# A fifth split place in the attention overlays, small sum jobs in the merge gates, and stored block sums, in a Strassen-Winograd decoder layer

## Chip, core and metric

The kernel runs on one core of one Trainium2 chip. The metric is the device time of one execution in microseconds. The engines are named as in the profile: PE (TensorE's matmuls), PEld (its weight loads), DVE (VectorE), ACT (ScalarE), POOL (GpSimd) and SP (SyncE, whose queue issues nearly all DMAs).

## What is computed

One decoder layer on 2048 tokens with 1024 features, in float32, batch and depth 1:

```python
mod = silu(c) @ w_ada + b_ada;  shift, scale, gate = split(mod, 3)
u = x * (1 + scale) + shift
q, k, v, a_gate, p_in, p_gate, m_a, m_p = split(u @ w_in)
a = (sliding_window_sink_attention(q, k, v, sinks, rel_bias) * silu(a_gate)) @ w_attn_proj
p = ((group_linear(multiscale_causal_pool(p_in), w_pool_mix) * pool_scale) * silu(p_gate)) @ w_pool_proj
y = ((sigmoid(m_a) * a + sigmoid(m_p) * p) @ w_out) * (1 + gate)
x = layer_norm(alpha * x + y, ln_gain, ln_bias)
```

There are 16 query heads of 64 and 2 key-value heads, a window of 128 tokens, and causal pools over 2, 4, 8 and 16 tokens.

## The kernel before

**Quads.** Every large matrix product is cut into quads: 256 output features by 1024 tokens (one chunk, `s` = 0 or 1), summed over 1024 input features. A quad is one step of the Strassen-Winograd scheme: seven block products instead of eight, named B11, T1, T2, B21, T3, B22, T4 after the set of the second operand that they read. A set is four tiles of 128 x 512, each split into a high and a low part that TensorE takes at full speed; a product is 4 x 3 matmuls of 512 columns (high by high, high by low, low by high, `mm3`, line 142), so 12 PE instructions. `sets` holds all seven sets of one operand in SBUF; when an operand is done, `turn_sets` (line 540) loads the next one's from DRAM and splits it, one set after another.

**Weights of a quad.** `Quad.load_w` (line 262) loads four blocks of 128 x 512 into a tile W and a fifth into A22. `sum1` (274), `mid` (277) and `late` (282) form sums and differences in W on POOL. Before its products a quad's blocks pass through four splits, stages F (products B11, T1), S (T2, B21), Th (T3, B22) and L (T4): ACT casts the high part (`split_part` part 0), DVE, or POOL for Th of unpaired quads, subtracts it for the low part (part 1). The parts stand in tiles `w_set`.

**The order of the work** is a table made by `plan` (line 352): 518 products in a row, and for each product which splits, loads and sums are issued ahead of it. F, S and Th need two places for `w_set` tiles, L one. A ring of four places serves all stages; a phase whose pools have `wx` places of its own uses those as well, and its splits may stand three products ahead instead of two (line 405). A part whose place is freed only by the product just ahead is put right at its own product (lines 418 and 419). Each engine executes its instructions in this program order. Small work is hung between products by `at`, `steps` and `defer` (lines 327 to 342), in ticks of one product.

**Phases.** For each chunk: the chunk start (`g0`, `g1`: keys and values, the first quads of q and gates, in pairs; products 0 to 27 and 175 to 202), the overlay (`o0`, `o1`: 13 unpaired quads, 91 products, 28 to 118 and 203 to 293, between whose matmuls `overlay` (746) sets the attention steps) and the merge gates (`e0`, `e1`: 8 paired quads, 56 products, 119 to 174 and 294 to 349, with the pooling by `pool_job`, 980). Then come the projections for chunk 0 and 1 (112 products) and the output product (56). `c` (line 203) hands out tiles for results from a ring of four, with `more` places where the phase has them.

**The attention step** (845) is 12 PE instructions: four scores (`lg`), four transposes (`pt`), four value products (`pv`); with a minimum, a scaling, a low part and two sums on DVE, two exponentials, a scaling, a cast and a copy on ACT.

**Small jobs.** `fold_parts` (1050) multiplies W_in's pool columns with the pool mix in chunk 0's start: 16 pieces of 12 matmuls, written to `wmix_d` through tiles of `c`. `sums_job` (945) forms the seven sets of u for chunk 1 in eight jobs (u_B, u_T in the profile) during chunk 0's overlay; `second_start` (1360) forms those of w_out times the gate in chunk 1's start with tiles `spare` of 128 x 1024 (`sums_to`, 224).

## Time and profile before

| | us |
|---|---|
| Median of 3 runs (lowest to highest) | 1837.79 (1834.65 to 1840.94) |
| The profiled execution's own time | 1841.62 |
| Its span, first to last instruction | 1839.8 |
| PE / DVE / ACT / POOL busy in it | 1705.4 / 1302.6 / 940.8 / 683.6 |
| Mean granted clock of PE | 0.972 |

Times in the profile are microseconds unless marked ns. A row of the timeline is start, duration, engine, operation with output<-inputs and shapes, and in brackets the engine's idle time before it with what ended that. In a group row the two numbers behind the bar are total busy time and mean ns of one, then the idle time before them. A row of the windows view is a stretch, its length, the busy time of each engine with the number of instructions, the granted clock, the DMA engines' mean busy share and GB/s. All helpers are called through one line, so every row says L56 and is told apart by its tiles.

### The profile page before, as it was taken

To read this page: it belongs to the slowest core of one execution; us is meant where nothing else is said; L and a number is where in the kernel's file an instruction comes from. 1 tells how busy PE (TensorE), PEld (TensorE's weight loads), DVE (VectorE), ACT (ScalarE), POOL (GpSimd) and SP (SyncE) were. 2 spreads that over 40 slices of the span, in tenths; PEclk is the share of its full clock that TensorE was granted. 3 is DMA by queue.
4 is the path that set the end of the run, shared out by engine and by line. 5 is a ranking of instruction groups with operands and counts; after the bars stand their busy time and mean duration, and the time that the engine had idled before them with its cause. 6 is when DMAs were issued, how large, how long until landed. Compare 5 with 4: busy or idle time off the path is not lost.

```text
span 1839.8 us, 24893 instructions
## 1 busy us (share of the span) xinstructions
PE 1705.4 (93%) x8061; PEld 1407.7 (77%) x8061; DVE 1302.6 (71%) x2309; ACT 940.8 (51%) x1796; POOL 683.6 (37%) x618
## 2 busy tenths in 40 slices
PE   6897799898989999989998999899999999999996
PEld 5686678777877887867886878688878888888785
DVE  5854578677763877757786877557786876879778
ACT  3543577666662435526675767434363444434452
POOL 3021345353534232473342444433232333323452
PEclk9899899999999999999999999999999999999998
DMA  8486646555533779595354544257785684778342
GB/s 332 139 264 214 177 153 190 185 179 188 169 129 129 233 237 349 193 334 176 123 166 139 172 130 150 99 163 227 237 306 202 235 284 158 251 247 290 137 149 103
DMA packets 223267, 365.13 MB, mean 198 GB/s; under 512 B 21776, under 2 KB 78880, under 8 KB 223136
## 3 DMA queue, kind: packets, MB, share of 16 engines
q1 hardware_dynamic: 221056, 359.55, 59.1%
q10 hardware_dynamic: 2048, 3.96, 0.7%
q8 instruction: 64, 1.05, 0.2%
q14 instruction: 67, 0.55, 0.1%
q0 software_dynamic: 32, 0.02, 0.0%
HBM read 235.50 MB, written 131.10 MB: 199 GB/s over the span
## 4 chain that ended last, share of the span: by engine, by line
PE 48%; DVE 14%; ACT 10%; issue 8%; DMA 7%; POOL 4%; SPq 1%; POOLq 0%; DVEq 0%; ACTq 0%
PE mm L56 29%; PE lg L56 9%; PE c L56 7%; DVE w_set L56 5%; ACT L L56 3%; ACT w_set L56 2%; DVE wide L56 2%; PE pv L56 2%; PE pt L56 1%; POOL W L56 1%; DVE L L56 1%; POOL st L56 1%; DMA qs<-q_d 1%; DVE ptl L56 1%; SPq L56 1%
## 5 line engine op out<-in xcount | busy, mean ns | idle before, releaser
L56 PE MATMUL mm<-set_B,w_set 128*128 128x512 f32 x2664 | 657.1, 393 | 4.8 <-DVE w_set L56 3.0
L56 PEld LDWEIGHTS mm<-set_B,w_set 128*128 128x128 f32 x2664 | 499.3, 190 | 110.8 <-DVE w_set L56 5.0
L56 PE MATMUL mm<-set_T,w_set 128*128 128x512 f32 x1824 | 480.0, 407 | 60.3 <-DVE w_set L56 38.5
L56 POOL TENSOR_TENSOR W<-W 128x512 f32<-128x512 f32 x216 | 315.6, 1476 | 464.8 <-DVE w_set L56 309.2
L56 PEld LDWEIGHTS mm<-set_T,w_set 128*128 128x128 f32 x1824 | 345.7, 195 | 155.1 <-DVE w_set L56 59.0
L56 DVE TENSOR_TENSOR w_set<-W,w_set 128x1024 fp32r<-128x1024 f32 x196 | 258.4, 1319 | 135.6 <-ACT w_set L56 110.1
L56 ACT CAST w_set<-W 128x1024 fp32r<-128x1024 f32 x222 | 232.2, 1047 | 196.5 <-POOL W L56 181.0
L56 POOL TENSOR_TENSOR W<-W,A 128x512 f32<-128x512 f32 x72 | 103.6, 1439 | 389.8 <-DMA A<-in_win_dram 187.6
L56 PE MATMUL c<-set_T,w_set 128*128 128x512 f32 x864 | 214.2, 397 | 8.4 <-DVE w_set L56 5.9
L56 PE MATMUL lg<-set_T,w_set 128*128 128x512 f32 x864 | 212.4, 394 | 4.8 <-ACT w_set L56 2.2
L56 PEld LDWEIGHTS c<-set_T,w_set 128*128 128x128 f32 x864 | 163.8, 191 | 46.2 <-DVE w_set L56 8.4
L56 PEld LDWEIGHTS lg<-set_T,w_set 128*128 128x128 f32 x864 | 163.0, 190 | 42.1 <-ACT w_set L56 3.1
L56 ACT ACTIVATE L<-L,nm 128x257 f32<-128x257 f32 (+1 forms) x256 | 126.8, 498 | 19.4 <-DVE nm L56 19.1
L56 DVE CUSTOM_DVE_ANT_0 L<-lg,bt,nsink 128x256 f32<-128x256 f32 (+1 forms) x256 | 111.0, 470 | 18.5 <-PE lg L56 16.9
L56 DVE TENSOR_SCALAR L<-L,sm 128x256 f32<-128x256 f32 (+1 forms) x128 | 114.3, 893 | 4.5
L56 ACT ACTIVATE L<-L,sm 128x256 f32<-128x256 f32 (+1 forms) x128 | 64.2, 502 | 101.6 <-DVE sm L56 101.6
L56 DVE TENSOR_TENSOR ptl<-pt,pth 128x512 fp32r<-128x512 f32 (+1 forms) x128 | 85.9, 671 | 34.5 <-ACT pth L56 33.7
L56 ACT CAST pth<-pt 128x512 fp32r<-128x512 f32 (+1 forms) x128 | 72.2, 564 | 56.2 <-PE pv L56 55.8
L56 PEld LDWEIGHTS lg<-kk,qs 128*128 128x128 f32 x512 | 79.2, 194 | 25.0 <-issue 10.4
L56 ACT ACTIVATE sig<-mm 128x512 f32<-128x512 f32 x76 | 45.4, 598 | 96.9 <-PE mm L56 86.0
L56 PE MATMUL lg<-kk,qs 128*128 128x256 f32 (+1 forms) x512 | 84.6, 289 | 9.7 <-DMA qs<-q_d 8.0
L56 DVE TENSOR_TENSOR w_set<-A,w_set 128x512 fp32r<-128x512 f32 x74 | 61.4, 830 | 34.1 <-ACT w_set L56 19.1
(205 smaller groups left out, 2026.0 us busy)
## 6 DMA issues: line engine op xcount, KB each, us to landing
W<-in_win_dram SPq DMA_DIRECT2D x40, 512.0 KB, 5.6
qs<-q_d SPq DMA_DIRECT2D x128, 128.0 KB, 4.0
W<-in_win_dram SPq DMA_DIRECT2D x46, 256.0 KB, 4.5
A<-in_win_dram SPq DMA_DIRECT2D x42, 256.0 KB, 5.5
ag_d<-sig SPq DMA_DIRECT2D x32, 256.0 KB, 3.9
q_d<-q_hi SPq DMA_DIRECT2D x32, 256.0 KB, 3.5
q_d<-q_lo SPq DMA_DIRECT2D x32, 256.0 KB, 3.6
pg_d<-sig SPq DMA_DIRECT2D x32, 256.0 KB, 3.9
```

What stands on the lines that cost most here:

```text
L56: return lambda *args, **kw: self.tc.keep_in_program_order(op(*args, **kw))
```

## The change

1. The overlays' pools get one `w_set` place of their own (`wx=1`), so `plan` uses five and issues splits up to three products ahead.
2. The eight jobs for u move from chunk 0's overlay to its merge gates, every 4.5 products; the sums of w_out become eight such jobs of half the width in chunk 1's merge gates, every 5.5 products, and leave chunk 1's start. `ux` gets two tiles.
3. For 31 of the quads chunk 0 stores the sum of `sum1` and the second difference of `mid` in `sums_d` (two stores of 256 KB each); chunk 1's quad of the same weights loads both in one DMA of 512 KB in place of one block and leaves the two POOL operations out.
4. The fold runs in 16 consecutive products, from the tenth on, and its result tiles come from ring `x`; the banks of the value transposes are swapped.
5. The results' ring has five tiles in chunk 0's merge gates and four in chunk 1's (six before), and six in chunk 1's start (four before), whose `spare` ring has five instead of seven.

What moves on DVE, in chunk 0's overlay at product T2 of the quad ag[6] (the row `mm<-mm,p` is the sum that follows T2; ISA is the minimum with its readout; `w_set<-W` is the low part of stage S). Before:

```order
L56 SCALAR_TENSOR_TENSOR q_lo<-mm,q_hi 128x512
L56 TENSOR_TENSOR w_set<-W,w_set 128x1024
L56 RECIPROCAL sm<-sm 128x2
L56 TENSOR_SCALAR L<-L,sm 128x256
L56 ISA L,nm<-lg,bt,nsink 128x256
L56 ISA nm 128x1
L56 ISA L,nm<-lg,bt,nsink 128x256
L56 ISA nm 128x1
L56 TENSOR_TENSOR ptl<-pt,pth 128x512
L56 TENSOR_TENSOR st<-pv,o_4159 64x128 x2
L56 TENSOR_TENSOR mm<-mm,p_4130 128x512
```

Now, two attention steps earlier, at the result of the quad before:

```order
L56 TENSOR_TENSOR st<-pv,o_3919 64x128 x2
L56 SCALAR_TENSOR_TENSOR q_lo<-mm,q_hi 128x512
L56 TENSOR_TENSOR w_set<-W,w_set 128x1024
L56 RECIPROCAL sm<-sm 128x2
L56 TENSOR_SCALAR L<-L,sm 128x128
```

The low part of S stood one attention step ahead of the sum behind T2, that is, at T2 itself; now two more steps lie between, and the place where it stood holds none.

What moves on SP, in chunk 0's merge gates behind the weights of the third group's first quads (`pg_d`, `mp_d` and `ma_d` hold gates, `vb` and `pin_` belong to the pooling, DMAHW and the engine names are the semaphores waited for). Before:

```order
L56 DMA A_5842<-in_win_dram 128x512 [waits DMAHW3_49]
L56 DMA pg_d<-sig 128x512 [waits DMAHW4_49,DVE_49]
L56 DMA vb<-px_d 128x528 [waits DMAHW5_49,DVE_49]
L56 DMA pg_d<-sig 128x512 [waits DMAHW6_49]
L56 DMA pin_T_109<-st 128x512 [waits DMAHW7_49,DVE_49]
L56 DMA pg<-pg_d 128x512 [waits DMAHW0_49]
```

Now:

```order
L56 DMA A_5767<-in_win_dram 128x512 [waits DMAHW5_49]
L56 DMA u_T_82<-ux 128x256 [waits DMAHW6_49,Pool_49]
L56 DMA u_T_86<-ux 128x256 [waits DMAHW7_49,Pool_49]
L56 DMA u_T_84<-ux 128x256 [waits DMAHW0_49,Pool_49]
L56 DMA u_B_80<-ux 128x256 [waits DMAHW1_49,Activation_49]
L56 DMA u_B_83<-ux 128x256 [waits DMAHW2_49,Activation_49]
L56 DMA u_B_85<-ux 128x256 [waits DMAHW3_49]
L56 DMA ux<-in_xt_dram 128x2x256 [waits DMAHW6_49,DMAHW7_49,DMAHW4_49,DMAHW0_49]
L56 DMA ux<-in_xt_dram 128x2x256 [waits DMAHW5_49]
L56 DMA pg_d<-sig 128x512 [waits DVE_49]
L56 DMA sums_d<-W 128x512 [waits Pool_49]
L56 DMA vb<-px_d 128x528 [waits DVE_49]
```

A job's six stores and two loads stand between the weights and the gates' stores, and the first load waits for the landing of the three u_T stores just ahead. Counted in the same order, from three rows ahead of the stage's first gate load (`pg<-pg_d`) to the first load of the next operand's sets, SP issues 178 DMAs with 41.0 MB in chunk 0's merge gates (96 with 26.8 MB before) and 164 with 39.3 MB in chunk 1's (96 with 26.9).

What moves on PE, at the end of chunk 0's start (`pv<-spare` and `pt<-spare` are folds). Before:

```order
L56 MATMUL lg<-set_T_560,w_set 128x512 x12
L56 MATMUL mm<-set_B_569,w_set 128x512 x12
L56 MATMUL pv<-spare,room_w 128x256 x12
L56 MATMUL c_970<-set_T_560,w_set 128x512 x12
L56 MATMUL pt<-spare,room_w 128x256 x12
L56 MATMUL mm<-set_B_569,w_set 128x512 x12
L56 MATMUL pv<-spare,room_w 128x256 x12
L56 MATMUL lg<-set_T_642,w_set 128x512 x12
L56 MATMUL pt<-spare,room_w 128x256 x12
L56 MATMUL c_970<-set_T_642,w_set 128x512 x12
```

Now:

```order
L56 MATMUL lg<-set_T_561,w_set 128x512 x12
L56 MATMUL pv<-spare,room_w 128x256 x12
L56 MATMUL mm<-set_B_570,w_set 128x512 x12
L56 MATMUL pt<-spare,room_w 128x256 x12
L56 MATMUL c_959<-set_T_561,w_set 128x512 x12
L56 MATMUL pv<-spare,room_w 128x256 x12
L56 MATMUL mm<-set_B_570,w_set 128x512 x12
L56 MATMUL pt<-spare,room_w 128x256 x12
L56 MATMUL lg<-set_T_635,w_set 128x512 x12
L56 MATMUL c_959<-set_T_635,w_set 128x512 x12
```

The gap after the third fold of four is gone and the last fold ends one product earlier.

The diff, without the removed `sums_to` and `second_start` and without repeated forms:

```diff
+    sums_d = dp.tile([36, P, 2, CH], F32, name="sums_d")
...
-        def __init__(self, srcs, consume):
-            self.srcs, self.consume = srcs, consume
+        def __init__(self, srcs, consume, sums=None, again=False):
+            self.srcs, self.consume, self.sums, self.again = srcs, consume, sums, again
...
-            q.dma_start(x[:, 2, :], self.srcs[1][:, 0:CH])
+            if self.again:
+                q.dma_start(x[:, 1:3, :], self.sums)
+            else:
+                q.dma_start(x[:, 2, :], self.srcs[1][:, 0:CH])
...
             e.tensor_tensor(x[:, 1, :], x[:, 1, :], x[:, 0, :], ALU.subtract)
-            e.tensor_tensor(x[:, 2, :], x[:, 0, :], x[:, 2, :], ALU.subtract)
+            if not self.again:
+                e.tensor_tensor(x[:, 2, :], x[:, 0, :], x[:, 2, :], ALU.subtract)
+
+        def keep_sum(self, n):
+            if self.sums is not None and not self.again:
+                sp.dma_start(self.sums[:, n, :], self.w[:, 1 + n, :])
...
             q.mid(pool)
+            defer(2, lambda q=q: q.keep_sum(1))
...
-                    z.sum1()
+                    if not z.again:
+                        z.sum1()
+                        defer(1, lambda z=z: z.keep_sum(0))
...
-            vtp = bank(("pt", "pv")[t]).rearrange("p (b a d) -> p b a d", b=NB, a=2)
+            vtp = bank(("pv", "pt")[t]).rearrange("p (b a d) -> p b a d", b=NB, a=2)
...
-        return Quad((win[TQ + m], win[TQ + m + 1]), consume)
+        return Quad((win[TQ + m], win[TQ + m + 1]), consume, sums_d[1 + m // 2], s == 1)
...
-    def sums_job(ph, i, c):
+    def sums_job(ph, store, i, c, load, scale):
...
-            u = job["u"] = ph.t.tile([P, 4, C2], F32, tag="ux", bufs=1, name="ux")
+            u = job["u"] = ph.t.tile([P, 4, C2], F32, tag="ux", bufs=2, name="ux")
...
+    def input_sums(ph, first):
...
+        for n in range(8):
+            steps(first, 1 + 4.5 * n, sums_job(ph, u1_d, n // 2, n % 2, load, scale))
+
+    def output_sums(ph, first):
...
+        def scale(u, k):
+            dve.tensor_tensor(u, u, row[0], ALU.mult)
+
+        for c in range(2):
+            at(first + 1 + 22 * c, lambda c=c: gate_cols(c))
+            for i in range(4):
+                steps(first, 1 + 5.5 * (4 * c + i), sums_job(ph, wo_d, i, c, load, scale))
...
-            st = ph.c("st").rearrange("p (m e d) -> p m e d", m=2, e=2)
+            st = ph.own("st").rearrange("p (m e d) -> p m e d", m=2, e=2)
...
-            first = base + 4 + 5 * g
+            first = base + 6 + 4 * g
...
-                    at(p - 2, lambda g=g: split_mix(g))
+                    at(p - 1, lambda g=g: split_mix(g))
...
-            if s == 0:
-                for n in range(8):
-                    steps(first, 1 + 11 * n, sums_job(ph, n // 2, n % 2))
...
+            (output_sums if s else input_sums)(ph, phase["first"])
...
-            phase(Pools("g1", spare=7, wx=2), start, second_start)
-        phase(Pools(f"o{s}", pv=2), alone, middle(s))
-        phase(Pools(f"e{s}", pg=2, st=8, more=2, wx=2), end, finish_chunk(s, ain_d[0] if s else u1_d))
+            phase(Pools("g1", spare=5, wx=4, more=2), start, second_start)
+        phase(Pools(f"o{s}", pv=2, wx=1), alone, middle(s))
+        phase(Pools(f"e{s}", pg=2, st=8, more=1 - s, wx=2), end, finish_chunk(s, ain_d[0] if s else u1_d))
```

`sums_job` keeps its ten steps over nine products: load at 0, scaling at 3 and 4, stores of B11, B21 and B22 at 5, differences on POOL at 5, 7 and 8, the other stores at 6 and 9.

72 lines of the change are left out of this document (21 added, 51 removed).

## The prediction

> **What bounds the kernel now.** I read the windows view first, cut at the program's stages: chunk start (first row), overlay of chunk 0, merge gates of chunk 0, then the same three of chunk 1.
>
> ```profile
> core 0: us, PE busy (x) PEld busy (x) DVE busy (x) ACT busy (x) POOL busy (x), PEclk, DMA share, GB/s
> 23.80:172.70 148.90, 126.00 (x619) 104.43 (x620) 90.67 (x150) 66.24 (x112) 17.48 (x11) 0.92 0.67 223
> 172.70:572.70 400.00, 360.18 (x1830) 297.98 (x1829) 268.98 (x676) 253.09 (x596) 179.63 (x194) 0.96 0.56 172
> 572.70:725.40 152.70, 152.50 (x673) 125.89 (x671) 112.64 (x140) 63.50 (x92) 44.36 (x39) 1.00 0.71 237
> 725.60:814.30 88.70, 81.10 (x346) 64.82 (x347) 61.70 (x57) 36.47 (x51) 52.90 (x32) 0.98 0.78 274
> 814.30:1203.40 389.10, 360.04 (x1862) 299.44 (x1861) 271.08 (x672) 246.04 (x579) 157.55 (x163) 0.97 0.47 150
> 1203.40:1356.00 152.60, 152.59 (x674) 126.00 (x672) 112.65 (x140) 63.49 (x92) 43.05 (x31) 1.00 0.74 238
> ```
>
> The merge gates are PE at its limit: 673 matmuls in 152.70 us, 0.227 us each and no idle. That is the price of one 512-column matmul, and 12 of them, one product, cost 2.72. An overlay has 91 products, 1092 matmuls, 247.8 us. Its other PE instructions (1830 - 1092 = 738 and 1862 - 1092 = 770) come in attention steps of 12. The timeline of PE gives a step as 434.68 - 433.30 = 1.38 us:
>
> ```profile
> 433.30 0.64 PE L56 MATMUL lg<-kk,qs 128*128 128x256 f32 x4
> 434.68 1.54 PE L56 MATMUL mm<-set_B,w_set 128*128 128x512 f32 x6
> ```
>
> So the overlays need 247.8 + 61.5 x 1.38 = 332.7 and 247.8 + 64.2 x 1.38 = 336.4 us, and take 67.3 and 52.7 more. The waits of PE in each (total, times, longest) name the cause, first three rows chunk 0, last two chunk 1:
>
> ```profile
> PE mm L56 <- DVE w_set L56: 20.7, 12, 2.6
> PE mm L56 <- ACT w_set L56: 8.2, 8, 2.1
> PE lg L56 <- DMA qs<-q_d: 6.9, 2, 6.7
> PE mm L56 <- DVE w_set L56: 17.9, 10, 2.8
> PE mm L56 <- ACT w_set L56: 6.2, 7, 2.1
> ```
>
> PE waits for the weights' high and low parts, about once per quad. The timelines of PE, DVE and POOL show one case, the T2 product of ag[6]:
>
> ```profile
> 420.90 3.37 PE L56 MATMUL mm<-set_T,w_set 128*128 128x512 f32 x14
> 426.81 0.50 PE L56 MATMUL mm<-set_T,w_set 128*128 128x512 f32 x1 [2.53 <-DVE w_set L56]
> 424.61 2.15 DVE L56 TENSOR_TENSOR w_set<-W,w_set 128x1024 fp32r<-128x1024 f32 x1
> 424.41 1.26 POOL L56 TENSOR_TENSOR st<-st 128x512 f32<-128x512 f32 x1
> ```
>
> DVE begins the low part at 424.61, after the product before (T1) has let go of its place, and PE resumes 0.05 us after it ends.
>
> **The fifth place.** The order shows that this low part now stands two attention steps earlier on DVE, so the 2.53 us go, as do the other waits for w_set. What is late next? Two quads of the windows view, one without and one with the wait:
>
> ```profile
> 262.80:290.90 28.10, 27.78 (x154) 23.38 (x153) 23.48 (x57) 20.48 (x52) 12.72 (x15) 1.00 0.56 164
> 411.95:444.95 33.00, 29.82 (x153) 24.89 (x153) 25.15 (x63) 21.44 (x54) 12.60 (x14) 0.95 0.60 202
> ```
>
> By the prices a quad needs 84 x 0.227 + 70/12 x 1.38 = 27.1 us. The first loses 1.0, the second 5.9, of which only 2.5 is the named idle: the clock fell to 0.95 and matmuls beside a gap stand alone. The Trainium skill, TensorE: Matmul & The Clock Gate, Part 1, lets the clock fall to half only after an idle window of about 3.4 us; by it waits of at most 2.8 us would cost no clock. The 0.95 beside a 2.53 us wait says otherwise, so I go by the whole excess; what the page's reading would give is a rival below.
>
> Not recoverable: the wait for qs, whose loads the change leaves where they stand:
>
> ```profile
> 200.40 1.19 PE L56 MATMUL lg<-kk,qs 128*128 128x256 f32 x4 [6.75 <-DMA qs<-q_d]
> ```
>
> The four scores behind it take 1.19 instead of the 0.64 at 433.30, so the clock was low too: I set 9 us in chunk 0, 2 in chunk 1. That leaves 58 and 51. After the change a quad still loses something, since DVE is busy 23.5 to 25.2 us of 27.1. From the rows: at least 1.0; if DVE can't be used over 23.48 / 28.10 = 84%, a quad with 25.15 takes 30.1, a loss of 3.0. I take 1.2, near the quad that ran, over 13 quads 15.6 per overlay: gains of 42 and 35, **77 us**. Ends: 109 with no loss, 55 with 2.1 (midway).
>
> **Chunk start, the fold.** Its products now follow one another without a gap and its result tiles leave the ring of four that q's and the gates' results use. PE around the last folds, and one wait of ACT among them:
>
> ```profile
> 148.33 0.50 PE L56 MATMUL pt<-spare,room_w 128*128 128x256 f32 x2 [1.39 <-ACT room_w L56]
> 160.05 0.63 ACT L56 ACTIVATE sig<-p 128x512 f32<-128x512 f32 x1 [5.12 <-DMA q_d<-q_hi]
> 161.21 2.93 PE L56 MATMUL pv<-spare,room_w 128*128 128x256 f32 x12 [7.93 <-ACT st L56]
> 168.37 1.70 PE L56 MATMUL pt<-spare,room_w 128*128 128x256 f32 x12 [1.24 <-ACT st L56]
> 169.91 2.91 PE L56 MATMUL c<-set_T,w_set 128*128 128x512 f32 x12
> ```
>
> From 148.33 to 169.91 (21.6 us) stand three folds and two products, which cost 3 x 1.54 (169.91 - 168.37) + 2 x 2.72 = 10.1 undisturbed. Some 11.5 are lost, 13 with the wait ahead, and ACT waited there for a store of a tile of that ring to land. I take **10**; ends 0 (the queue that delays the stores still waits for the gate sums) and 13.
>
> **Chunk 1's start.** The sums of w_out leave it. It needs 28 x 2.72 = 76.3 and takes 88.70. DVE's timeline, and PE's wait:
>
> ```profile
> 786.77 1.23 DVE L56 TENSOR_TENSOR spare<-spare,cb 128x1024 f32<-128x1024 f32 x1 [7.23 <-DMA spare<-in_wout_dram]
> 787.92 1.22 DVE L56 TENSOR_TENSOR w_set<-W,w_set 128x1024 fp32r<-128x1024 f32 x1
> PE c L56 <- DVE w_set L56: 3.8, 1, 3.8
> ```
>
> DVE stood for w_out's load with splits behind it. That goes: **6** of the 12 (the idle and a low clock after it); ends 3 and 9.
>
> **The merge gates take the small jobs.** Prices of what moves, and of what the stored sums spare:
>
> ```profile
> L56 POOL TENSOR_TENSOR ux<-ux 128x256 f32<-128x256 f32 x32 | 25.6, 811 | 3.0 <-ACT ux L56 2.9
> L56 ACT ACTIVATE ux<-ux,mod 128x512 f32<-128x512 f32 x16 | 12.8, 807 | 0.0
> L56 DVE TENSOR_TENSOR spare<-spare,cb 128x1024 f32<-128x1024 f32 x8 | 12.6, 1596 | 9.6 <-DMA spare<-in_wout_dram 9.6
> L56 DVE TENSOR_TENSOR w_set<-W,w_set 128x1024 fp32r<-128x1024 f32 x196 | 258.4, 1319 | 135.6 <-ACT w_set L56 110.1
> ```
>
> In chunk 0's gates POOL goes from 44 to 70 of 152.7 us and ACT from 64 to 76: covered. In chunk 1's, DVE goes from 112.7 to 125; and beside POOL a split took 2.15 instead of 1.32, so 32 small POOL operations can lengthen DVE's work by up to 32 x 0.83 = 27, to 152 of 152.6. The Trainium skill, SBUF — State Buffer, Who interferes with whom, calls this an exclusive port that a two-input DVE operation and GpSimd hold in turn; the 2.15 agrees.
>
> The DMAs are the nearer limit. Up to the first load of the next sets (46 products, 125 us) the order has 178 DMAs with 41.0 MB in chunk 0's gates where it had 96 with 26.8: 327 GB/s for 214. The densest stretch before, and an ordinary one:
>
> ```profile
> 680.00:698.00 18.00, 18.00 (x81) 14.92 (x80) 13.01 (x15) 8.70 (x13) 8.61 (x7) 1.00 0.73 248
> 716.00:734.00 18.00, 15.95 (x67) 11.94 (x65) 12.23 (x13) 8.40 (x12) 6.54 (x4) 1.00 1.05 401
> ```
>
> 401 GB/s is reached, with PE 2 us short. So 327 fits, with little spare, and the sets' turn follows at once. SP is also held: a job's load goes into a tile whose stores were issued just before, so SP stands for a landing, with weight loads queued behind it; those stand three products (8.2 us) ahead of their split, which is the cover. The results' ring shrinks from six tiles to five and four; a tile is stored two products after it is made and its landing takes 3.9 us:
>
> ```profile
> ag_d<-sig SPq DMA_DIRECT2D x32, 256.0 KB, 3.9
> ```
>
> That is 9.3 of the 10.9 us that four products give. And DVE, as at 786.77, can again stand for w_out, now with three products of cover instead of two. All of this is hidden on average and not in every burst: I take **+4** for each of the two stages with what follows it; ends 0 and +18.
>
> **Stored sums.** Chunk 1 saves two POOL operations in each of 31 quads; POOL is not what PE waits for, so 0. Chunk 0 stores 62 tiles of 256 KB, spread over its stages: 0, with a rival below. The swapped banks of the value transposes and the smaller rings of chunk 1's start change no count and no order that PE waits for: 0.
>
> **Sum.** The profiled execution took 1841.62 us (span 1839.8, 1.8 around it; 3.8 above the median of the runs shown, inside their scatter): 1841.6 - 77 - 10 - 6 + 8 = **1757**. Below 0.3%, 5.5 us, a change can't be told from none.
>
> **Rivals.**
> DVE takes PE's place in the overlays: 2.1 lost per quad, gain 55 instead of 77: **1779**. For it: 84% at the quickest quad. Against: that quad still kept up. 0.15.
> The merge gates starve: PE is short by 2 in 18 us, as at 716, over 2 x 153 us: 34 instead of 8: **1783**. 0.12. Both: **1805**, 0.04.
> Only the named idle returns (28.9 and 24.1, less the 31 kept): gain 22, **1812**. It is the clock page's reading as well; the quad at 411.95 speaks against it. 0.04.
> No loss per quad and no price in the gates: 1841.6 - 109 - 12 - 8 = **1713**. 0.04.
> The splits wait for their own inputs instead, so the place gives nothing: 1841.6 - 16 + 8 = **1834**. 0.03.
> Slower: in chunk 0 the difference that overwrites a stored sum must wait on POOL until the store has landed, with the second split's input behind it. If PE saw that landing in all 31 quads, 31 x 3.9 = 121: 1757 + 121 = **1878**. It decides from 85 / 31 = 2.7 us per quad. Against: two to three products lie between store and difference in the overlays, and the second split stands four products later in the paired stages. 0.03.
> The forecast keeps 0.55.
>
> **Numbers.** Range 1730 (1.0 lost per quad or less, no price in the gates) to 1793 (past the two single rivals). Faster by over 0.3%: 0.55 + 0.15 + 0.12 + 0.04 + 0.04 + 0.04 and a third of the 0.03 = 0.95; within 0.02; slower 0.03.
>
> **What would show it.** Right: overlays of about 358 and 354 us with under 5 us of PE waiting for w_set in each; the chunk start about 139; chunk 1's start about 83; the gates 153 to 160 with DMA near 0.95. DVE as the bound shows as PE waiting for nm, ptl or w_set with DVE over 84% busy there; starving gates as PE idle there behind DMAs of W or A; the slower case as POOL's W<-W waiting for sums_d. I am wrong if the overlays keep more than 370 us or the gates exceed 165.

## The result, and the profile after

The changed kernel takes 1810.52 us in the median of four runs (1806.00 to 1817.08), beside 1836.22 of the kernel before on the same chip: a ratio of 0.986, interval 0.9822 to 0.9898. It is faster, by some 26 us where 80 were forecast, and lies above the range (1730 to 1793). The profiled execution is the slowest of the four, 1817.08 us, its span 1815.3.

The windows view of the changed kernel, cut at the same products as before (to some 0.4 us): chunk 0's start, overlay and merge gates, then chunk 1's (columns as in the prediction's first rows). The last row is one quad of chunk 0's overlay, ag[6], which took 33.00 us before.

```profile
23.60:168.70 145.10, 129.10 (x618) 107.31 (x619) 90.28 (x152) 69.21 (x115) 16.54 (x12) 0.92 0.71 242
168.70:534.40 365.70, 346.89 (x1830) 293.32 (x1830) 262.69 (x675) 239.55 (x577) 160.81 (x162) 0.98 0.56 174
534.40:731.30 196.90, 166.86 (x674) 132.95 (x672) 111.43 (x140) 74.71 (x109) 70.47 (x69) 0.90 0.79 264
731.30:811.70 80.40, 78.33 (x345) 63.92 (x346) 46.97 (x50) 38.22 (x53) 19.27 (x13) 1.00 0.54 187
811.70:1169.40 357.70, 345.05 (x1862) 294.08 (x1861) 263.80 (x670) 243.62 (x578) 125.80 (x134) 1.00 0.52 168
1169.40:1332.00 162.60, 154.64 (x675) 125.55 (x673) 122.80 (x156) 63.67 (x93) 56.48 (x48) 0.99 0.90 304
395.30:423.80 28.50, 27.58 (x153) 23.57 (x152) 23.71 (x63) 20.74 (x52) 11.52 (x13) 1.00 0.64 215
```

Against the rows of before:

| stage | before | forecast | after | difference | forecast difference |
|---|---|---|---|---|---|
| chunk 0's start | 148.9 | 139 | 145.1 | -3.8 | -10 |
| chunk 0's overlay | 400.0 | 358 | 365.7 | -34.3 | -42 |
| chunk 0's merge gates | 152.7 | 157 | 196.9 | **+44.2** | +4 |
| chunk 1's start | 88.7 | 83 | 80.4 | -8.3 | -6 |
| chunk 1's overlay | 389.1 | 354 | 357.7 | -31.4 | -35 |
| chunk 1's merge gates | 152.6 | 157 | 162.6 | +10.0 | +4 |

The six differences sum to -23.6, and the span fell by 24.5. The overlays gave 65.7 of the 77 that were forecast. Two thirds of the miss (40 of 61 us) stand in chunk 0's merge gates, where PE hardly idled before (152.50 of 152.70 us busy). PE's waits there now (total, times, longest):

```profile
PE mm L56 <- ACT w_set L56: 27.9, 5, 11.0
PE mm L56 <- DVE w_set L56: 1.2, 3, 0.5
```

There are five waits for the high part of the weights, up to 11.0 us long, and a granted clock of 0.90 beside them. One of them is followed here from end to end, in the third group of pairs. First PE's timeline, the T3 products of the group before, at which the weights of the third group's two quads are due (in the order, their loads stand ahead of the first and the third of these rows), and the wait itself:

```profile
601.95 2.88 PE L56 MATMUL lg<-set_T,w_set 128*128 128x512 f32 x12
604.67 2.88 PE L56 MATMUL mm<-set_B,w_set 128*128 128x512 f32 x12
607.39 2.88 PE L56 MATMUL c<-set_T,w_set 128*128 128x512 f32 x12
...
640.26 5.89 PE L56 MATMUL mm<-set_B,w_set 128*128 128x512 f32 x12 [10.98 <-ACT w_set L56]
```

Then SP's issues:

```profile
610.74 1.08 SPq L56 DMA_DIRECT2D W<-in_win_dram  x2
611.86 0.62 SPq L56 DMA_DIRECT2D A<-in_win_dram  x1
...
613.80 1.87 SPq L56 DMA_DIRECT2D u_T<-ux  x3
621.09 1.20 SPq L56 DMA_DIRECT2D ux<-in_xt_dram  x2
...
622.98 1.02 SPq L56 DMA_DIRECT2D W<-in_win_dram  x2
624.04 0.67 SPq L56 DMA_DIRECT2D A<-in_win_dram  x1
...
630.29 0.32 SPq L56 DMA_DIRECT2D sums_d<-W  x1
```

And POOL's and ACT's timelines:

```profile
618.85 1.26 POOL L56 TENSOR_TENSOR W<-W,A 128x512 f32<-128x512 f32 x1 [8.06 <-DMA vb<-px_d]
635.43 2.48 POOL L56 TENSOR_TENSOR W<-W 128x512 f32<-128x512 f32 x2 [14.63 <-DMA sums_d<-W]
637.87 1.26 POOL L56 TENSOR_TENSOR W<-W,A 128x512 f32<-128x512 f32 x1
639.16 1.04 ACT L56 CAST w_set<-W 128x1024 fp32r<-128x1024 f32 x1 [14.13 <-POOL vb L56]
```

Read backwards: PE waits for the cast at 639.16, that for the sum of the pair's second quad at 637.87, and that stands on POOL behind the first quad's differences (635.43), which waited 14.63 us for a stored sum to land. The sum itself was ready at 620.1; its store was issued at 630.29, 10.2 us later. Apart from that, both quads' weights came late: SP issued them 8.8 (610.74 - 601.95) and 15.6 us (622.98 - 607.39) behind their products. Between 615.67 (613.80 + 1.87) and 621.09 SP issued nothing: the job's load at 621.09 goes into the tile of stores just ahead. (The stretch of SP's order that is shown with the change is the same thing one group earlier: it stands behind the weights of the second group, not of the third.) There are thus two suspects, SP's queue and the stored sums.

### The profile page after: what moved, and what is told of

Same layout as the page of the kernel before. It is cut to its first block, busy times and chain, and to the rows that moved or that the text cites. A ratio compares the mean times of both kernels' runs of the same rounds, so it can differ in the third digit from the quotient of the medians.

```text
span 1815.3 us, 25023 instructions
## 1 busy us (share of the span) xinstructions
PE 1693.8 (93%) x8061; PEld 1406.1 (77%) x8061; DVE 1277.1 (70%) x2317; ACT 940.8 (52%) x1796; POOL 612.1 (34%) x572
## 5 line engine op out<-in xcount | busy, mean ns | idle before, releaser
L56 PE MATMUL mm<-set_B,w_set 128*128 128x512 f32 x2664 | 672.8, 399 | 38.7 <-ACT w_set L56 34.7
L56 PEld LDWEIGHTS mm<-set_B,w_set 128*128 128x128 f32 x2664 | 506.5, 193 | 152.3 <-ACT w_set L56 38.1
L56 POOL TENSOR_TENSOR W<-W 128x512 f32<-128x512 f32 x185 | 273.7, 1490 | 657.7 <-DVE w_set L56 371.8
L56 PE MATMUL mm<-set_T,w_set 128*128 128x512 f32 x1824 | 456.1, 397 | 4.3 <-POOL w_set L56 3.2
L56 DVE TENSOR_TENSOR w_set<-W,w_set 128x1024 fp32r<-128x1024 f32 x196 | 254.4, 1299 | 179.5 <-ACT w_set L56 160.1
L56 PE MATMUL c<-set_T,w_set 128*128 128x512 f32 x864 | 210.2, 391 | 4.5 <-DVE w_set L56 2.4
L56 ACT ACTIVATE L<-L,nm 128x257 f32<-128x257 f32 (+1 forms) x256 | 126.9, 498 | 24.6 <-DVE nm L56 24.0
L56 POOL TENSOR_TENSOR W<-W,A 128x512 f32<-128x512 f32 x41 | 60.4, 1474 | 210.1 <-DMA A<-in_win_dram 89.2
L56 PE MATMUL lg<-kk,qs 128*128 128x256 f32 (+1 forms) x512 | 84.3, 287 | 28.2 <-DVE nm L56 16.5
L56 DVE TENSOR_TENSOR ptl<-pt,pth 128x512 fp32r<-128x512 f32 (+1 forms) x128 | 85.7, 669 | 25.1 <-ACT pth L56 24.5
L56 DVE TENSOR_SCALAR L<-L,sm 128x256 f32<-128x256 f32 (+1 forms) x128 | 96.9, 757 | 4.5
L56 POOL TENSOR_TENSOR ux<-ux 128x256 f32<-128x256 f32 x64 | 65.7, 1039 | 54.9 <-ACT sig L56 14.6
```

Source lines behind the costliest of these rows:

```text
L56: return lambda *args, **kw: self.tc.keep_in_program_order(op(*args, **kw))
```

## The experiments

Theory A puts the loss on the stored sums, theory B on SP's queue held by the jobs, theory C on the DMA engines. Ratios are to the kernel before on the same chip, with 95% intervals; the stages are from the windows views, in us, of one profiled execution each. Kernels that share a stage's code show how far such figures scatter: chunk 0's overlay with the fifth place and the stored sums took 359.8 to 365.7 us in the five kernels changed, jobs_55, wide_jobs, mid_later and weights_on_act. "Late" is the greatest lateness of the weight loads for the third and the fourth group of chunk 0's gates (four loads), worked out like the 15.6 above.

| kernel | ratio (interval) | overlay 0 | gates 0 | late | overlay 1 | gates 1 |
|---|---|---|---|---|---|---|
| before | 1 | 400.0 | 152.7 | 0.0 | 389.1 | 152.6 |
| changed | 0.986 (0.9822 to 0.9898) | 365.7 | 196.9 | 15.6 | 357.7 | 162.6 |
| no_sums | 0.9736 (0.9709 to 0.9762) | 356.7 | 174.4 | 15.3 | 361.3 | 168.9 |
| sums_on_act | 0.982 (0.9792 to 0.9849) | 362.4 | 184.9 | 16.3 | 359.4 | 163.5 |
| jobs_55 | 0.9754 (0.9718 to 0.979) | 365.1 | 179.7 | 11.1 | 360.4 | 162.6 |
| u_in_overlay | 0.9814 (0.978 to 0.9847) | 399.8 | 154.7 | 0.6 | 358.6 | 161.4 |
| no_sums_jobs_55 | 0.9661 (0.9635 to 0.9686) | 356.8 | 158.7 | 6.5 | 359.7 | 167.9 |
| wide_jobs | 0.9749 (0.9728 to 0.9769) | 362.2 | 174.1 | 4.4 | 360.8 | 161.5 |
| mid_later | 0.9757 (0.973 to 0.9784) | 361.5 | 180.4 | 17.2 | 359.3 | 161.3 |
| weights_on_act | 0.9857 (0.982 to 0.9893) | 359.8 | 191.1 | 9.5 | 359.7 | 167.3 |
| no_sums_weights_act | 0.9775 (0.9751 to 0.98) | 358.5 | 173.0 | 10.6 | 360.1 | 176.5 |
| no_sums_55_weights_act | 0.9741 (0.9715 to 0.9767) | 358.8 | 166.4 | 8.8 | 360.2 | 175.8 |
| gate_sums | 0.9645 (0.9619 to 0.967) | 356.0 | 163.6 | 7.1 | 359.8 | 163.0 |
| gate_sums_wide | 0.964 (0.9613 to 0.9666) | 356.4 | 161.7 | 5.3 | 360.0 | 161.4 |
| no_sums_wide | 0.9658 (0.9636 to 0.9679) | 356.2 | 160.0 | 4.4 | 359.8 | 167.6 |
| no_sums_wide_both | 0.9637 (0.9612 to 0.9661) | 358.8 | 159.7 | 4.4 | 359.6 | 163.4 |

### Which of the two: sums, jobs, or both

**no_sums**, the changed kernel with

```diff
-            self.srcs, self.consume, self.sums, self.again = srcs, consume, sums, again
+            self.srcs, self.consume, self.sums, self.again = srcs, consume, None, False
```

> The changed kernel without the stored sums: nothing goes to sums_d, and chunk 1 forms its sums and differences on POOL as it did before. Chunk 0's merge gates took 197.0 us for 153.1 before. Theory A (the difference on POOL waits for a stored sum's landing, and the sum of the pair's other quad stands behind it on POOL): these gates fall to 153 to 160 us and the time to about 1772. Theory B (SP stands for the landing of a job's stores ahead of the job's load, and weight loads are late behind it, whatever is stored): the gates stay at 185 or more, the time at 1800 or more. Theory C (the gates carry more bytes than the DMA engines move): in proportion to the bytes left, gates near 190, time near 1803. Chunk 1 with its POOL operations back: within 4 us of the changed kernel by all three.

Chunk 0's start, overlay and gates in the windows view:

```profile
23.80:165.10 141.30, 126.33 (x619) 105.43 (x620) 93.07 (x153) 69.17 (x115) 18.47 (x12) 0.94 0.70 239
165.10:521.80 356.70, 342.01 (x1829) 289.69 (x1828) 262.64 (x673) 239.37 (x577) 159.62 (x161) 1.00 0.52 159
521.80:696.20 174.40, 160.82 (x674) 129.52 (x672) 113.52 (x140) 74.70 (x109) 72.25 (x70) 0.96 0.81 274
```

Half of the 44 us went, where A said nearly all and B nearly none. The weight loads stayed as late as they were (15.3 us), and what that does is seen at the same place of the third group: PE still waits 3.81 us there, for a sum that waited 5.56 us on POOL for the block A of the late load. Each theory has half. Chunk 1's gates missed the 4 us that all three allowed: they take 168.9 us for 162.6, so the stored sums spare some 6 us there, where the prediction had nothing.

**u_in_overlay**, the other half taken out (the jobs every 11 products with one tile, as before):

```diff
+            if s == 0:
+                input_sums(ph, first)
...
-            (output_sums if s else input_sums)(ph, phase["first"])
+            if s:
+                output_sums(ph, phase["first"])
...
-        phase(Pools(f"o{s}", pv=2, wx=1), alone, middle(s))
+        phase(Pools(f"o{s}", pv=2, **({"wx": 1} if s else {})), alone, middle(s))
```

> The changed kernel with the jobs of u back in chunk 0's overlay (every 11 products, one tile) and that overlay without its fifth place, since the tile takes its room; the stored sums stay everywhere. Chunk 0's overlay: 395 to 402 us by all theories. Its merge gates: theory A by itself (stores of sums are enough) 185 or more, time near 1835; theory B, and an interplay of stored sums with a queue held by jobs, 153 to 160, time 1800 to 1806; theory C, with the jobs' bytes gone, 153 to 160 as well.

```profile
165.00:564.80 399.80, 358.76 (x1829) 296.58 (x1828) 269.33 (x675) 252.34 (x594) 180.13 (x194) 0.96 0.60 188
564.80:719.50 154.70, 153.02 (x674) 126.04 (x672) 110.00 (x140) 63.62 (x93) 43.21 (x40) 1.00 0.77 257
```

Without the jobs the gates are back at 154.7 with every stored sum in place, and the weights are on time. This is what B, and an interplay of both, had put there; A by itself falls. So the jobs alone cost 21.7 us (174.4 - 152.7), the sums alone 2.0 (154.7 - 152.7; 4.7 in sums_only below), and both together 44.2: some 20 us exist only where both are. The overlay, without its place, is back at 399.8.

**sums_only**, the kernel before with part 3 of the change (`Quad`, `keep_sum`, the sums handed to the quads) and nothing else:

> The kernel before with the stored sums alone (stores in chunk 0, one load of 512 KB and no sum or second difference on POOL in chunk 1). The prediction's term: 0, every stage of before within 3 us. The rival of the prediction (the difference on POOL waits for the landing): up to 121 us slower, in the stages of chunk 0. From the other runs: merge gates of chunk 0 near 155 without jobs, chunk 0's overlay up to 9 longer, chunk 1's overlay up to 4 shorter; time within 10 of before.

Chunk 0's overlay and gates, and chunk 1's overlay and gates:

```profile
171.40:571.30 399.90, 360.14 (x1830) 296.88 (x1829) 268.81 (x676) 253.31 (x596) 179.72 (x194) 0.96 0.60 189
571.30:728.70 157.40, 153.87 (x675) 125.77 (x673) 110.99 (x140) 63.77 (x93) 42.87 (x39) 1.00 0.76 256
814.50:1205.80 391.30, 363.21 (x1862) 302.90 (x1860) 270.68 (x671) 246.26 (x579) 124.01 (x136) 0.96 0.50 160
1205.80:1358.90 153.10, 152.70 (x674) 126.07 (x672) 111.39 (x140) 63.74 (x93) 22.06 (x16) 1.00 0.74 241
```

The ratio is 1.0017, interval 0.9993 to 1.004: nothing that can be told from none. POOL's work in chunk 1's overlay falls from 157.6 to 124.0 us and that overlay isn't shorter; POOL is not what PE waits for. By itself the part is worth what was forecast, 0, but for chunk 0's gates, which take 157.4 us, 4.7 more, where 3 were allowed and about 155 us expected.

### How the sums and the jobs act on each other

**mid_later** lets the pair's other sum go ahead of the difference that waits, and stores the second difference two products later:

```diff
-            q.mid(pool)
-            defer(2, lambda q=q: q.keep_sum(1))
+            if q.pair:
+                defer(2, lambda q=q: q.mid(pool))
+            else:
+                q.mid(pool)
+            defer(4 if q.pair else 2, lambda q=q: q.keep_sum(1))
```

> The changed kernel with the two differences of a paired quad one product later on POOL, behind the sum of the pair's other quad instead of ahead of it, and the store of the second difference two products later; jobs and stored sums as in the changed kernel. Chunk 0's merge gates lost 44 us there and 21 without stored sums. If the stored sums cost what they do because the waiting difference holds the other quad's sum behind it on POOL: gates 170 to 180 us, time 1785 to 1793. If the sums cost by what they add to SP's queue: gates 190 or more, time 1803 or more.

POOL's waits in chunk 0's merge gates, total, times and longest, the row of the changed kernel and then the same row here:

```profile
POOL W L56 <- DMA sums_d<-W: 39.7, 3, 14.6
```

```profile
POOL W L56 <- DMA sums_d<-W: 4.7, 3, 4.2
```

```profile
529.00:709.40 180.40, 161.95 (x674) 128.09 (x673) 113.48 (x140) 74.77 (x109) 73.45 (x70) 0.97 0.85 285
```

Two instructions moved by one product take 35 of the 39.7 us off this row of waits, and 16.5 of the some 20 us that exist only where sums and jobs meet; 180.4 is just above the 170 to 180 that were expected, far from the 190 of the other reading. The weights are as late as ever (17.2), and POOL now waits for them instead (33.4 us for the block A). The bytes and the number of DMAs are those of the changed kernel. So the sums' price in the gates is mostly what the waiting difference held behind it.

**sums_on_act** leaves that order as it is and issues the stores elsewhere:

```diff
-                sp.dma_start(self.sums[:, n, :], self.w[:, 1 + n, :])
+                act.dma_start(self.sums[:, n, :], self.w[:, 1 + n, :])
```

> The changed kernel with the stores of the sums issued from ACT's queue in place of SP's; bytes and jobs unchanged. Theory A with the delay in SP's queue (a sum's store was issued up to 10 us after the sum was made): chunk 0's merge gates fall from 197 to 155 to 165 us, time about 1775. Theory A with the delay in the landing itself: gates at 190 or more. Theory B: weights still late, gates at 180 or more, time at 1795 or more. Theory C: gates unchanged at 197, time 1810.

```profile
529.10:714.00 184.90, 164.59 (x675) 130.49 (x674) 112.32 (x140) 74.60 (x109) 68.54 (x70) 0.94 0.83 281
```

It gives 12 us back, a part only; 184.9 us lies where B had put it (180 or more). POOL's waits for sums_d fall from 39.7 to 3.1 us, so it was the place in SP's queue that made a sum land late. The weights are as late as ever (16.3), and ACT, which makes the splits, now stands for the jobs' landings (7.2 us for u_B and 5.0 for u_T ahead of a split). That the whole loss would go with the delay in SP's queue was not borne out.

### What holds SP's queue

**jobs_55** spaces the jobs wider, **wide_jobs** makes four of the eight:

```diff
-            steps(first, 1 + 4.5 * n, sums_job(ph, u1_d, n // 2, n % 2, load, scale))
+            steps(first, 1 + 5.5 * n, sums_job(ph, u1_d, n // 2, n % 2, load, scale))
```

> The changed kernel with the jobs of u every 5.5 products in chunk 0's merge gates in place of 4.5, as those of w_out stand in chunk 1's, so that a load comes two products after the stores of the tile that it reuses and not right behind them. Theory B: SP no longer stands, gates fall from 197 to 155 to 165 us, time about 1775. Theory A: the store of a sum is a little less late, gates 180 to 195, time 1795 to 1809. Theory C: the same bytes in the same stage, 195 or more.

```diff
-        C2, job = CH // 2, {}
+        C2, job = CH // (1 if store is u1_d else 2), {}
...
-        for n in range(8):
-            steps(first, 1 + 4.5 * n, sums_job(ph, u1_d, n // 2, n % 2, load, scale))
+        for n in range(4):
+            steps(first, 1 + 11 * n, sums_job(ph, u1_d, n, 0, load, scale))
```

> The changed kernel with four jobs of u of full width every 11 products in one tile of 8 KB, in place of eight of half width every 4.5 in two tiles of 4 KB: the same bytes and the same room, half the DMAs on SP (32 for 64) and half the places where SP stands for a landing; the stored sums stay. If SP's queue holds the weights by the number of what stands in it, gates 155 to 168 us, time 1772 to 1785; if bytes hold it, near the 180 of the run with wider spacing or above, time 1795 or more.

The gates with wide jobs (179.7 us with the wider spacing):

```profile
527.80:701.90 174.10, 159.23 (x675) 127.95 (x673) 115.93 (x140) 71.84 (x101) 68.71 (x54) 0.97 0.85 294
```

Both missed the ranges set for them (155 to 165, 155 to 168), and jobs_55 came where A alone would have put it (some 180). The stored sums are still in them, so by themselves they can't tell. But the lateness answers: 15.6 us with eight jobs every 4.5 products, 11.1 every 5.5, 4.4 with four wide ones at equal bytes. **no_sums_jobs_55**, the edits of no_sums and of jobs_55 together, acts on both suspects:

> The changed kernel without the stored sums and with the jobs of u every 5.5 products. Of the 44 us that chunk 0's merge gates lost, 21 stayed without the stored sums and 26 with the wider spacing. If the two are separate losses (each a part of the 44), little is left: gates 153 to 160, time about 1775. If the jobs' own number of DMAs on SP holds the weights whatever the spacing, gates stay near 170 and the time near 1788.

```profile
520.80:679.50 158.70, 154.08 (x675) 125.70 (x673) 113.76 (x140) 74.50 (x108) 74.87 (x70) 1.00 0.86 284
```

It takes 158.7 us, inside the 153 to 160 that were expected if the two are separate losses, and the ratio is 0.9661. Theory C falls: these gates move 284 GB/s where the starved ones moved 264, and mid_later moves the changed kernel's bytes at 285. Nor do the loads land much later: a load of 512 KB into W takes 6.7 us from issue to landing in the changed kernel's gates (median) for 6.3 before. The weights are late because they are issued late.

**weights_on_act** tries another way past SP's queue, and with it **no_sums_weights_act** and **no_sums_55_weights_act**, the same edit on the kernels without stored sums:

```diff
-                    z.load_w(ph)
+                    z.load_w(ph, act if ph.name[0] == "e" else sp)
...
-                    z.load_last(ph, z.own)
+                    z.load_last(ph, z.own, act if ph.name[0] == "e" else sp)
```

> The changed kernel with the weight loads of both merge gates (three DMAs a quad) issued from ACT's queue in place of SP's; jobs, stored sums and bytes as in the changed kernel. Weight loads were issued 8.8 to 15.6 us late in chunk 0's gates. If that lateness is the jobs' whole price there, and the stored sums' price is separate: gates from 197 to 172 to 180 us, time about 1790, chunk 1's gates from 162 to 155. If the loads are no earlier to land, since the DMA engines are what is full, or ACT stands for a free tile with splits behind: gates 190 or more, time 1803 or more.

> The changed kernel without stored sums, and with the weight loads of both merge gates from ACT's queue; jobs every 4.5 products as in the changed kernel. Without stored sums alone chunk 0's gates took 174.4 us and chunk 1's 168.9. If the weights' lateness behind the jobs on SP is the cause of what was left: 153 to 157 and 153 to 160, time 1760 to 1767. If the jobs cost by their bytes or by their work on POOL, ACT and DVE: 168 or more in chunk 0's, time 1783 or more.

> The changed kernel without stored sums, with jobs of u every 5.5 products and the weight loads of both merge gates from ACT's queue. If the weights' lateness is what is left in the gates: 153 to 156 us in chunk 0 (158.7 with those loads on SP), 153 to 160 in chunk 1 (167.9), time 1758 to 1766. If not: within 3 of the 1775 with those loads on SP.

None gives what SP's queue as the whole cause would: 191.1, 173.0 and 166.4 us came. The first two lie where the other readings had put them (190 or more, 168 or more); the last fits neither and is slower than with the loads on SP, and chunk 1's gates are slower too. One of ACT's waits in chunk 0's gates of weights_on_act, which the changed kernel hasn't got:

```profile
ACT sig L56 <- DMA u_T<-ux: 16.1, 3, 6.5
```

A gate's activation (sig) has no use for u_T. But the weight load ahead of it on ACT waits for a landing: in this program's order the semaphores go round by eight, DMAHW5, 6, 7, 0, 1 and so on over both queues, and a DMA waits for the one whose semaphore it takes over, that is, until the eighth one ahead of it has landed. The order of this kernel's ACT, the loads of the second group's second quad:

```text
L56 DMA W<-in_win_dram 128x512 [waits DMAHW4_49,DMAHW0_49,Activation_49]
L56 DMA W<-in_win_dram 128x2x512 [waits DMAHW7_49]
L56 DMA A_5767<-in_win_dram 128x512 [waits DMAHW3_49]
```

So two queues stand for the jobs' stores now, one of them with the splits in it. The Trainium skill, DMA: Bandwidth & Descriptors, Issuing engines are not separate DMA queues, says that issuing from several engines saves only the sequencer's time to initiate the DMA; the 191.1 us for 196.9 agree.

If eight under way is the limit, the number of DMAs counts. **no_sums_wide**, the edits of no_sums and of wide_jobs, halves the number of the jobs' DMAs at equal bytes (72 to 36; the 64 and 32 of the expectation of wide_jobs leave out one store a job):

> The changed kernel without stored sums and with four wide jobs of u every 11 products in one tile of 8 KB. Each DMA waits for the landing of the eighth DMA ahead of it, so the number of DMAs counts, on whichever queue they stand. If that number is what is left without stored sums: weight loads at most 5 us late, chunk 0's gates 153 to 157 us (174.4 with narrow jobs every 4.5 products, 158.7 every 5.5), time 1766 to 1774. If bytes or the engines' work count: 160 or more, time 1776 or more.

```profile
522.10:682.10 160.00, 155.48 (x674) 126.86 (x672) 118.02 (x140) 72.08 (x101) 69.04 (x54) 0.99 0.86 294
```

**no_sums_wide_both** does it in chunk 1's gates too, with the whole row of the gate in one tile:

```diff
-        C2, job = CH // 2, {}
+        C2, job = CH, {}
...
-                steps(first, 1 + 5.5 * (4 * c + i), sums_job(ph, wo_d, i, c, load, scale))
+            steps(first, 1 + 12 * i, sums_job(ph, wo_d, i, 0, load, scale))
...
-        phase(Pools(f"e{s}", pg=2, st=8, more=1 - s, wx=2), end, finish_chunk(s, ain_d[0] if s else u1_d))
+        phase(Pools(f"e{s}", pg=2, st=8 - s, more=1 - s, wx=2), end, finish_chunk(s, ain_d[0] if s else u1_d))
```

> The same with four wide jobs of w_out every 12 products in chunk 1's gates too (the ring st of the pooling has seven tiles there in place of eight, to make room for the full row of the gate). Chunk 1's gates took 168.9 and 167.9 us without stored sums. If the number of DMAs is the cause there as well: 155 to 161, time 1758 to 1766. If the work of DVE on w_out and its order is the cause, or the ring of seven costs as much: 165 or more, time as no_sums_wide.

```profile
520.60:680.30 159.70, 155.56 (x674) 126.90 (x672) 118.00 (x140) 72.26 (x101) 68.55 (x54) 0.99 0.86 294
1120.30:1283.70 163.40, 154.16 (x674) 125.68 (x672) 124.91 (x148) 63.61 (x93) 70.01 (x45) 0.99 0.87 293
```

With half the DMAs the lateness is 4.4 us, inside the 5 expected, and the gates go from 174.4 to 160.0: 14 of the 21.7 us that the jobs cost by themselves. The time, 1777.15, and the 160.0 lie at the edge of the other reading (1776 or more, 160 or more). That the number is the cause is not shown: no_sums_jobs_55, with all 72 DMAs, takes as little, 158.7. What the two edits have in common is that a job's load no longer comes right behind the stores of its tile (SP's waits for u_T fall from 13.1 us in no_sums to 4.0 and below), and that the jobs are spread over 44 products for 36; no run tells these apart. The seven us that stay may be the jobs' work or their bytes. In chunk 1's gates only 4 of some 15 us go (163.4 for 167.6), between the two readings, and what holds the rest is open.

### The other terms, one at a time

**place_only_chunk1**, one line of the change on the kernel before:

```diff
-        phase(Pools(f"o{s}", pv=2), alone, middle(s))
+        phase(Pools(f"o{s}", pv=2, **({"wx": 1} if s else {})), alone, middle(s))
```

> The kernel before with one thing of the change: the place of its own for w_set in chunk 1's overlay (chunk 0's has no room for it beside the jobs' tile). If the place carries the overlay's gain alone, as the prediction has it: that overlay falls from 389 to 354 to 360 us, the time by 29 to 35 (about 1805 on a chip where before takes 1838), no other stage moves. If the gain came from the shorter work of POOL (the stored sums): 380 or more, time within 10 of before.

```profile
815.40:1176.90 361.50, 346.41 (x1862) 293.80 (x1861) 268.30 (x672) 245.10 (x579) 163.49 (x164) 1.00 0.51 162
```

**fold_only**, part 4 of the change on the kernel before:

```diff
-            vtp = bank(("pt", "pv")[t]).rearrange("p (b a d) -> p b a d", b=NB, a=2)
+            vtp = bank(("pv", "pt")[t]).rearrange("p (b a d) -> p b a d", b=NB, a=2)
...
-            st = ph.c("st").rearrange("p (m e d) -> p m e d", m=2, e=2)
+            st = ph.own("st").rearrange("p (m e d) -> p m e d", m=2, e=2)
...
-            first = base + 4 + 5 * g
+            first = base + 6 + 4 * g
...
-                    at(p - 2, lambda g=g: split_mix(g))
+                    at(p - 1, lambda g=g: split_mix(g))
```

> The kernel before with the fold's part of the change alone: 16 products in a row, results in ring x, the banks of the value transposes swapped. The prediction's term: chunk start from 148.9 to about 139 us, time 10 less. The rival reading, that the loads and stores queued on SP hold the fold's stores and not the ring: chunk start 143 to 149, time 0 to 6 less.

Chunk 0's start, and the fold's wait in it:

```profile
23.70:165.30 141.60, 128.03 (x619) 106.66 (x620) 91.48 (x153) 68.23 (x114) 17.96 (x12) 0.93 0.70 239
```

```profile
155.50 2.93 PE L56 MATMUL pt<-spare,room_w 128*128 128x256 f32 x12 [4.02 <-ACT st L56]
```

The place alone takes 27.6 us off its overlay (389.1 to 361.5, just short of the 354 to 360 expected) and moves none of the other five stages by more than 1; the ratio is 0.9883, interval 0.9859 to 0.9907, which is 21 us by the medians where 29 to 35 were expected. The fold alone takes 7.3 off its stage, ratio 0.9956 (0.9941 to 0.9972): between the two readings, since one fold still waits 4.02 us for ACT's copy out of its bank. ACT's timeline says why: just ahead of that copy ACT stands 8.69 us, in its order, for the landing of `q_d<-q_hi`, with which a gate's result waits for its place in the ring.

### Is there a version that beats both

**gate_sums** and **gate_sums_wide** keep the stored sums for the eight quads of the merge gates alone (the other quads lose the two arguments), with the edit of mid_later, that of jobs_55 in the one and of wide_jobs in the other, and

```diff
-        kept = () if base + m == TAG else (sums_d[5 + (base + m - TAG) // 2], s == 1)
+        kept = () if name == "ag" or name != "mp" and m < 4 else (sums_d[5 + (base + m - TAG) // 2], s == 1)
```

> The changed kernel with three edits: stored sums for the eight quads of the merge gates alone, jobs of u every 5.5 products, and the differences of paired quads behind the other quad's sum. If the losses are as the runs so far have them: chunk start 140, chunk 0's overlay 357, its gates 155 to 162, chunk 1's overlay 360, its gates 162; time 1765 to 1772, below the 1775 of the run without any stored sum. If storing the gates' sums still costs what chunk 1's gates win by them: 1773 to 1780.

> The same as gate_sums, with the four wide jobs of u in place of the eight narrow ones. Weight loads were at most 4.4 us late with wide jobs in the second and third group, 11 with narrow ones every 5.5 products. If that lateness is what is left: gates 153 to 157 us, time 1762 to 1768. If wide jobs' longer POOL operations and the one tile take it back: gates 160 or more, time 1770 or more.

```profile
519.70:683.30 163.60, 156.28 (x675) 126.59 (x674) 112.92 (x140) 74.89 (x108) 79.18 (x69) 0.99 0.91 304
```

They take 1774.12 and 1773.09 us, not the 1765 to 1772 and 1762 to 1768 hoped for but what the second reading of each had: what chunk 1's gates win (163.0 and 161.4 for 167.9) chunk 0's lose. With no_sums_jobs_55, no_sums_wide and no_sums_wide_both (1775.03, 1777.15 and 1771.21) that makes five kernels between 0.9637 and 0.9661 whose intervals overlap; all beat the changed kernel's 0.986 clearly, none is shown the best.

## Why the prediction was wrong, step by step

**The overlays: right in the mechanism, short by 8 and 4.** The fifth place was to bring 42 and 35, and 34.3 and 31.4 came; alone in chunk 1 it brought 27.6. What is left in chunk 0's overlay is headed by DVE, as the prediction said:

```profile
PE lg L56 <- DVE nm L56: 9.0, 11, 2.1
PE lg L56 <- DMA qs<-q_d: 5.7, 2, 3.3
PE lg L56 <- DMA kk<-k_d: 2.4, 1, 2.4
PE mm L56 <- POOL w_set L56: 1.6, 1, 1.6
```

DVE's and ACT's w_set, 28.9 us before, are gone, POOL's has 1.6 left, and DVE's own step nm comes next, with DVE busy 23.71 of 28.50 us (83%) in ag[6]. The rival that had DVE as the bound at 84% has the right name and too high a price: this quad lost 1.4 us, not 3.0. Of chunk 0's shortfall of 8 us the stored sums explain a part: with them that overlay took 359.8 to 365.7 us in five kernels, the changed one being the slowest, and without them 356.2 to 358.8 in six. The quickest of these is 23.5 above the prediction's 332.7, where it had 24.6. Which wait of PE the sums lengthen there is not shown, and on the kernel before they cost that overlay nothing (399.9 for 400.0).

**The whole excess, not the named idle: right.** PE's idle (span less busy) fell by 21.0 us in chunk 0's overlay (39.8 to 18.8) and by 16.4 in chunk 1's (29.1 to 12.7), and 28.3 more came back as PE's own busy time, at clocks of 0.98 and 1.00 for 0.96 and 0.97. The Trainium skill, TensorE: Matmul & The Clock Gate, Part 1, puts the fall of the clock behind an idle window of about 3.4 us, and by that rule waits of at most 2.8 us would have cost no clock. (The same Part also tells of a kernel in which frequent short idles made the clock swing, so the prediction's reading of it was a narrow one.) The 33.00 us quad at 0.95 that became 28.50 at 1.00 says that here they did.

**The fold: over by 6.** 10 was taken; alone it brought 7.3, in the changed kernel 3.8. The step that failed is that leaving the ring would free ACT's copy: the tiles left it, but the copy stands behind another instruction that still waits for that ring (8.69 us in fold_only, 10.03 in the changed kernel, 5.12 before), and PE waits 4.02 and 5.36 us for it. The prediction said that the queue still could delay the stores and set the low end there; the value it took left little for it. The stored sums take some 3 us more: with them in all quads this stage took 141.4 to 145.3 us, without them 138.1 to 142.2.

**Chunk 1's start: 8.3 for 6.** The wait that the prediction named is gone: PE's 3.8 us for DVE's w_set and DVE's 9.6 us for w_out are in this stage's waits before and not after. But no run takes this part alone, and the list of the change leaves out that this stage's splits got four places of their own for two (`wx=4` in the diff); what that brings isn't shown.

**The merge gates: the step that failed.** The prediction's words were that weight loads "stand three products (8.2 us) ahead of their split, which is the cover", that 327 GB/s "fits", and +4 for each stage. It had named the place: "SP stands for a landing, with weight loads queued behind it". What it did not do is add up SP's time. Its own sign of being wrong, gates over 165, came at 196.9. SP's waits in chunk 0's gates:

```profile
SPq L56 <- POOL W L56: 24.2, 7, 6.4
SPq L56 <- DMA u_T<-ux: 14.2, 7, 5.1
SPq L56 <- DVE st L56: 12.9, 9, 3.4
SPq L56 <- POOL ux L56: 9.6, 7, 4.7
SPq L56 <- ACT ux L56: 6.1, 4, 5.0
```

The jobs' rows (ux and u_T) are 29.9 us, some 4 for each job, that of the stored sums (POOL W) 24.2. Such rows are not yet the price: before the change SP's waits in this stage sum to some 95 us, and no load was late, because SP had the time. The change took this time away. In the first 46 products SP's issues themselves take 86.6 us (180 DMAs of 0.48 us in the mean) where they took 40.8 (96 DMAs), so of the 125 us planned some 38 are left to stand in, and 84 were. The queue is in order, and what goes beyond is added to the lateness of all that follows: weights came 15.6 us late against a cover of 8.2. A mean rate (327 against 401 GB/s) could not show that; the rate that was in fact moved over the longer stage, 264, was below it. So the nearest rival, starving gates at 34 us for both, had the stage but neither the size in chunk 0 (44.2, and 10.0 in chunk 1) nor the mechanism: it priced a rate of bytes, and the loads land in 6.7 us for 6.3.

**The stored sums: right alone, wrong beside the jobs.** The rival for the slower side had the mechanism (POOL's difference waits for the landing) and was set aside for the paired stages because "the second split stands four products later". That split was not the one that waited: the sum of the pair's other quad stood behind the difference on POOL, and it was due at once. Moving the difference behind it took 35 us off POOL's wait for the stores and 16.5 us off the stage. In the overlays, which have no pairs, the argument held: POOL shows no such wait there. And "POOL is not what PE waits for, so 0" was too low for chunk 1's gates beside the jobs, which take 167.6 to 168.9 us without the stored sums and 161.3 to 163.5 with them (weight loads on SP, narrow jobs of w_out).

**DVE beside POOL**, bounded at up to 27 us in chunk 1's gates, is not seen: DVE was busy 122.80 us there, 10.2 more than before, where the w_out products alone were to add some 12. The exclusive port of the Trainium skill, SBUF — State Buffer, Who interferes with whom, is thus no large term in this stage.

In sum, of the 61 us between forecast (-85) and stages (-23.6), 40 are chunk 0's gates, 11 the overlays, 6 the fold, 6 chunk 1's gates, with 2 the other way in chunk 1's start. One sum of the prediction is off by itself: the rival of 1713 takes 12 and 8 where its ends read 13 and 9, which gives 1711; nothing hangs on it. What stays open: whether spacing or number is what counts in the jobs, the seven us that four wide jobs still cost chunk 0's gates, and most of the ten or fifteen in chunk 1's.

## What to carry to other kernels

When jobs are moved onto an in-order queue, count the queue's time, not the mean bytes per second: what its issues take, and how long it will stand (for tiles that were only just stored, and for the transfer whose semaphore is taken over). Compare the running sum with the lead of the loads queued behind. When an instruction gets a new wait, ask what stands behind it on its engine, not only who reads its result. Two additions that each cost little by themselves can cost much together when one delays what the other waits for, so measure them apart and together.

## What was not expected of the hardware

PE's waits cost more than their length: in chunk 0's gates of the changed kernel 30.0 us of idle (196.90 - 166.86) came with 14.4 us more of busy time than before (166.86 for 152.50) at a clock of 0.90, and the 12 matmuls behind the wait of 10.98 us took 5.89 us, where 12 take 2.88 in the undisturbed rows of the same view. The DMA engines moved more where PE waited less: 304 GB/s at a share of 0.90 in chunk 1's gates, 264 at 0.79 in chunk 0's.
